# Fourteen pairs of k tiles as seven products instead of twelve, in the down projection of a hybrid decoder layer

## The chip, the cores and the metric

The kernel runs on one core of one Trainium2 chip. The metric is the device time of one execution in microseconds, as the median of several runs. The profile is one more execution, taken with the hardware profiler.

## The reference

One decoder layer on 256 tokens of width 2048, all in float32: a token mixer (mLSTM and RWKV-7 side by side), cross-attention into 256 memory tokens, and a convolutional GeGLU. Only the end of the layer bears on the change:

```python
def conv_glu_ffn(h, w_up, conv_w, conv_b, w_down):
    u = h @ w_up
    uc = conv_b + sum(conv_w[j] * shift_right(u, CONV_WIDTH - 1 - j) for j in range(CONV_WIDTH))
    gate, up = split_cols(uc, (D_FF, D_FF))
    return (jax.nn.gelu(gate, approximate=True) * up) @ w_down
...
x = x + rms_norm(conv_glu_ffn(h, ffn_w_up[l], ffn_conv_w[l], ffn_conv_b[l], ffn_w_down[l]), ffn_post_norm[l])
```

`w_down` is 8192 x 2048. The product with it, (256 x 8192) by (8192 x 2048), is the down projection.

## The kernel before, in words

**Matmuls in parts.** float32 operands are split into a high part and a low part of the type fp32r, and a product is made of three matmuls: high by high, low by high, high by low. A weight tile of 128 x 1024 (a chunk) comes by DMA into `raw`; ScalarE copies it to `wh` (L448), VectorE subtracts to get `wl = raw - wh` (L520). The activations of the down projection, two k tiles at a time, go the same way into `as` (`asplit`, L1911): ScalarE the high part, VectorE the low one.

**The down projection.** It is two blocks, 0 and 1, each of 1024 output columns and 64 chunks; a chunk is one k tile of 128 rows. Four PSUM banks hold the output: two tiles of 128 tokens by two halves of 512 columns. A chunk is 4 banks x 3 matmuls = 12 matmuls with 512 columns each.

**Pairs.** At the places listed in `SEVEN` (L1906) two chunks k and k+1 are taken together. Their work is a 2 x 2 by 2 x 2 product of blocks (two token tiles, two k tiles, two column halves), 8 block products or 24 matmuls when done plainly. `seven_products` (L532) does it with 7 products of sums and differences, 21 matmuls. Some of its products add into the block's own four banks (`tm` in the profile), others into four further ones (`more`), which `join_sums` adds up once per block, after the last pair. In this text a pair is named by its first chunk: pair 12 is chunks 12 and 13.

**The preparation of a pair.** `prepare` (L452) is a generator of six steps. Its weights b11, b12 (chunk k) and b21, b22 (chunk k+1) lie in `sraw`, one place for all pairs. What it makes, and what the profile calls it:

- step 1: `t` first half = b22 + b12, and a difference of activations (VectorE; both written to `end`, since `sraw`, the sums and other scratch share one piece of memory of that name)
- step 2: b12 = b12 - b11 in place, and two more differences of activations (VectorE, `end`)
- step 3: `t` second half = b22 + b12 (VectorE), high part of the activations `sa` (ScalarE)
- step 4: `t` third part = b21 - second half, low part of `sa` (VectorE), high part of `ts` (ScalarE, 1024 columns)
- step 5: low part of `ts` (VectorE), high part of `t4` (ScalarE, 512 columns)
- step 6: low part of `t4` (VectorE); the profile prints `t4` as `t`

The seven products read, in order: `as` by the first chunk, `as` by the second, `sa` by the first, `sa` by the second, `sa` by `ts` twice, `as` by `t4`. Since b12 is changed in place, the split of the pair's first chunk into `wh` and `wl` comes after step 2.

**What sets the order.** All instructions are written out in program order, and each engine works through its own in that order. In `work` (L577), for every chunk i: `feed.lo` sees to it that `wh` and `wl` exist up to chunk i+3 (L607 and L613; for a pair up to i+4), `ax` splits the activations of the next two chunks, `pair_loads` (L481) starts the loads of the next pair's weights, two chunks before the pair in front of it, `ahead_of_pairs` (L492) runs one step of `prepare` per chunk (more if it is behind), and only then come the chunk's matmuls. A preparation is due to start at chunk k - 6 (L401). `wh` and `wl` have five buffers each, `as` two, `raw` four. The gain of the last norm is loaded at chunk 24 of block 0 (`load_gain`, L1966).

Of the kernel before, what the change touches and what calls it, by code (L numbers as in the profile page):

```python
# [148 lines left out]
def layer(tc, d, dbg=None):  # L149
    with ExitStack() as ctx:  # L150
        ctx.enter_context(tc.manual_schedule())
        _layer(ctx, tc, tc.nc, d, dbg or (lambda n, t: None))


def _layer(ctx, tc, nc, d, dbg):
# [127 lines left out]
    class Stat:  # L283


        def __init__(self, name, tag="ysb1", sq="au", home=None):
            self.name, self.tag, self.sq, self.home = name, tag, sq, home
            self.rc = cp.tile([P, 2], F32, name=name + "_c")
            self.n = 0
            self.done = False  # L290
# [91 lines left out]
    def block(kind, srcs, xs, evac, before=None, cols=512, pool_=None, pre=None, bankwise=False, tail=0,  # L382
              two=False, wide=None, seven=None):


        blocks.append(dict(kind=kind, srcs=srcs, xs=xs, evac=evac, before=before, cols=cols,
                           pool=pool_ or acc, pre=pre, task=None, bankwise=bankwise, tail=tail, two=two, wide=wide is not None, xw=wide,
                           seven=seven))
        return blocks[-1]

    class Feed:
        def __init__(self):
            a, g = blocks[0]["srcs"], blocks[1]["srcs"]
            self.src = a[:LEAD] + [c for p in zip(a[LEAD:], g) for c in p] + g[len(a) - LEAD:]
            self.src += [s for b in blocks[2:] for s in b["srcs"]]
            n, self.pairs, self.preps = sum(len(b["srcs"]) for b in blocks[:2]), {}, []
            for b in blocks[2:]:
                if b["seven"]:
                    for k in b["seven"]["at"]:
                        self.pairs[n + k], self.pairs[n + k + 1] = 0, 1  # L400
                        self.preps.append([n + k - 6, self.prepare(n + k, k), n + k, []])  # L401
                n += len(b["srcs"])
            self.raw, self.st, self.nd, self.ns, self.nl, self.nop = {}, {}, 0, 0, 0, 0

# [321 lines left out]
    def W(name, blk):  # L726
        return [d[name][blk, c] for c in range(d[name].shape[1])]
# [1175 lines left out]
        fu = block("fm", W("w_fw", f - 6), fu_xs(f), fw_evac(f), cols=256, wide=lambda k: M["fx"][:, :, k])  # L1903

    M["as"], M["a4"], M["sa"], M["ts"] = {}, [], [], []
    SEVEN = [12, 20, 30, 38, 48, 56], [10, 18, 28, 36, 46, 54]  # L1906

    def acpair(e):
        return M["ac"][e // 16][:, e % 16:e % 16 + 2] if e < 32 else M["ac"][2 + (e - 32) // 8][:, e % 8:e % 8 + 2]
# [1 line left out]
    def asplit(k):  # L1911

        if k not in M["as"]:
# [5 lines left out]
            for j in range(2):  # L1919
                M["as"][k + j] = (a[:, 0, j], a[:, 1, j])  # L1920
            if e in SEVEN[k // 64]:
                M["a4"].append([a[:, i].rearrange("p k (t s) -> p (k t) s", t=2) for i in range(2)])
        return M["as"][k]

    def ax(n):
        def xs(k):
            kk = n * 64 + k
            if kk == 58:
                side.need(fu["task"])
            if kk == 2:  # L1930
                room()
            if kk == 24:
                load_gain()
            if k % 2 == 0:
                asplit(kk)
                if kk + 2 < 128 and (k < 62 or n == 0):
                    asplit(kk + 2)
            return M["as"].pop(kk)
        return xs
# [117 lines left out]
    def fd_ready(n):  # L2057
        return lambda: side.need(fd[0]["task"] if n else fu["task"])

    fd = []  # L2060
    for n in range(2):
        fd.append(block("tm", W("w_fd", n), ax(n), fd_evac(n), cols=1024, pool_=acc if n else aux,
                        tail=4 if n else 0, seven=dict(at=SEVEN[n], pool=aux if n else acc, ready=fd_ready(n))))
    run()
# [102 lines left out]
```

## Time and profile before

| what | value |
|---|---|
| median of 3 runs | 1797.09 us (1797.02 to 1797.45) |
| the profiled execution | 1796.52 us |
| its span, first to last instruction | 1794.7 us |
| granted TensorE clock, mean | 0.999 |
| TensorE busy | 1785.2 us, 99% of the span |
| VectorE busy | 1395.6 us, 78% |
| ScalarE busy | 1076.7 us, 60% |
| DMA read from HBM | 347.01 MB, 195 GB/s over the span |

A row of a timeline reads: start in us from the span's start, length in us, engine, line of the kernel, operation, output<-input, shapes, count, and in brackets how long the engine stood idle before it and who ended that. PE is TensorE (PEld its weight loads), DVE VectorE, ACT ScalarE, SP the engine that issues DMAs. L191 is the helper through which every matmul goes and L68 the one through which most of the work of DVE and ACT goes, so those instructions are told apart by their tiles.

### The profile page before, as it was taken

Reading aid. Unit: us, or ns where it says so; the run is one execution under the profiler, and the core shown is the slowest. Engines: PE = TensorE matmul, PEld = TensorE weight load, DVE = VectorE, ACT = ScalarE, POOL = GpSimd, SP = SyncE. Lnnn points to the kernel's source line nnn. Section 1 sums busy time; section 2 is a strip of 40 time slices with the busy share of each in tenths; the row PEclk is TensorE's granted clock in tenths of the full one; section 3 lists DMA queues with packets and bytes.
Section 4 is the critical chain, followed back from the end, with each engine's and each line's share of the span. In section 5 each row is a group of like instructions: output and inputs, shape, how many; then the busy total and the mean of one; then the engine's idle time right before and its main releaser. Section 6 shows DMA issues by size and latency. Waiting matters only on the chain.

```text
span 1794.7 us, 30098 instructions
## 1 busy us (share of the span) xinstructions
PE 1785.2 (99%) x11778; PEld 1629.7 (91%) x11778; DVE 1395.6 (78%) x2020; ACT 1076.7 (60%) x1616; POOL 28.9 (2%) x51
## 2 busy tenths in 40 slices
PE   9999999999999999999999999999999999999998
PEld 9999988888888999999999999999999998888887
DVE  7869995766665767778878777877777778888887
ACT  7576454654554666677566667666655655556554
POOL 0100000000100000000000000000000000000000
PEclk9999999999999999999999999999999999999999
DMA  8755564454556676656666666666666676767664
GB/s 283 206 170 186 164 190 146 125 180 144 200 188 211 227 243 186 190 150 197 208 203 198 203 209 192 199 206 204 199 200 209 192 229 213 227 186 227 209 209 129
DMA packets 99134, 351.59 MB, mean 196 GB/s; under 512 B 10896, under 2 KB 13968, under 8 KB 98864
## 3 DMA queue, kind: packets, MB, share of 16 engines
q1 hardware_dynamic: 97888, 347.38, 61.3%
q8 instruction: 92, 1.51, 0.3%
q0 software_dynamic: 384, 1.18, 0.2%
q10 hardware_dynamic: 720, 1.12, 0.2%
q14 instruction: 50, 0.41, 0.1%
HBM read 347.01 MB, written 2.10 MB: 195 GB/s over the span
## 4 chain that ended last, share of the span: by engine, by line
PE 99%; DVE 0%; DMA 0%; ACT 0%; issue 0%; SPq 0%; DVEq 0%; ACTq 0%
PE fm L191 55%; PE tm L191 37%; PE more L191 2%; PE gram L191 0%; PE Y L191 0%; PE lv L191 0%; DMA op<-in_op_dram 0%; PE X L191 0%; PE num L191 0%; PE zwa L191 0%; PE U L191 0%; PE gramA L191 0%; PE xo L191 0%; PE zg L191 0%; PE Tn L191 0%; PE mT L1472 0%
## 5 line engine op out<-in xcount | busy, mean ns | idle before, releaser
L520 DVE TENSOR_TENSOR wl<-raw,wh 128x1024 fp32r<-128x1024 f32 (+1 forms) x617 | 741.5, 1218 | 128.6 <-ACT wh L448 125.9
L448 ACT CAST wh<-raw 128x1024 fp32r<-128x1024 f32 (+1 forms) x617 | 633.6, 1044 | 112.7 <-PE tm L191 61.7
L191 PE MATMUL fm<-fx,wh 128*128 128x512 f32 (+1 forms) x2240 | 672.8, 364 | 0.6 <-DVE fx L68 0.4
L191 PE MATMUL fm<-fx,wl 128*128 128x256 f32 x2048 | 558.3, 273 | 0.0
L191 PEld LDWEIGHTS fm<-fx,wh 128*128 128x128 f32 x2240 | 409.3, 190 | 49.9 <-DVE fx L68 1.0
L191 PEld LDWEIGHTS fm<-fx,wl 128*128 128x128 f32 x2048 | 393.3, 192 | 0.0
L191 PE MATMUL tm<-wh,as 128*128 128x512 f32 x856 | 254.8, 379 | 0.0
L191 PE MATMUL tm<-wh,hx 128*128 128x512 f32 (+1 forms) x832 | 243.9, 378 | 1.4 <-ACT hx L68 1.4
L191 PEld LDWEIGHTS tm<-wh,as 128*128 128x128 f32 x856 | 161.7, 189 | 23.2 <-DVE as L68 0.3
L68 ACT COPY ul<-fm 128x256 f32<-128x256 f32 x128 | 44.9, 373 | 225.5 <-PE fm L191 225.5
L191 PE MATMUL fm<-hx,wh 128*128 128x256 f32 x1024 | 174.5, 277 | 0.0
L191 PEld LDWEIGHTS tm<-wh,hx 128*128 128x128 f32 x832 | 151.0, 189 | 21.8 <-POOL wh L507 1.6
L191 PE MATMUL tm<-wl,as 128*128 128x512 f32 x428 | 162.2, 379 | 0.0
L191 PEld LDWEIGHTS fm<-hx,wh 128*128 128x128 f32 x1024 | 155.6, 192 | 1.1
L191 PE MATMUL tm<-wl,hx 128*128 128x512 f32 (+1 forms) x416 | 152.5, 373 | 0.4 <-DVE wl L520 0.3
L68 DVE TENSOR_TENSOR us<-fm,ul 128x256 f32<-128x256 f32 x128 | 48.5, 420 | 131.2 <-ACT ul L68 131.2
L191 PE MATMUL fm<-hx,wl 128*128 128x256 f32 x512 | 140.8, 275 | 0.0
L68 ACT CAST as<-ac 128x512 fp32r<-128x512 f32 x64 | 39.4, 617 | 118.8 <-PE tm L191 118.8
L191 PEld LDWEIGHTS fm<-hx,wl 128*128 128x128 f32 x512 | 98.3, 192 | 0.0
L191 PEld LDWEIGHTS tm<-wl,as 128*128 128x128 f32 x428 | 80.9, 189 | 11.5
L191 PEld LDWEIGHTS tm<-wl,hx 128*128 128x128 f32 x416 | 77.5, 189 | 11.2 <-DVE wl L520 0.5
L191 PE MATMUL fm<-mg,wh 128*128 128x512 f32 (+1 forms) x320 | 84.9, 340 | 0.0
(406 smaller groups left out, 2114.8 us busy)
## 6 DMA issues: line engine op xcount, KB each, us to landing
raw<-in_w_fw_dram SPq DMA_DIRECT2D x232, 512.0 KB, 4.3
raw<-in_w_in_dram SPq DMA_DIRECT2D x160, 512.0 KB, 3.7
raw<-in_w_fd_dram SPq DMA_DIRECT2D x104, 512.0 KB, 4.1
raw<-in_w_br_dram SPq DMA_DIRECT2D x32, 512.0 KB, 4.2
raw<-in_w_mw_dram SPq DMA_DIRECT2D x24, 512.0 KB, 4.8
raw<-in_w_fu_dram SPq DMA_DIRECT2D x24, 512.0 KB, 4.0
end<-in_w_fd_dram SPq DMA_DIRECT2D x24, 512.0 KB, 3.6
raw<-in_w_mo_dram SPq DMA_DIRECT2D x8, 512.0 KB, 4.1
```

Of the source, the lines that this page charges most:

```text
L68: return f(out, *a, **k)
L191: pe.matmul(out, lhsT, rhs, start=start, stop=stop, skip_group_check=True)
L448: nc.scalar.copy(o, v)
L520: nc.vector.tensor_sub(o, v, h)
```

## The change

```diff
                     for k in b["seven"]["at"]:
                         self.pairs[n + k], self.pairs[n + k + 1] = 0, 1
-                        self.preps.append([n + k - 6, self.prepare(n + k, k), n + k, []])
+                        last = self.preps[-1][2] if self.preps else 0
+                        self.preps.append([max(n + k - 6, last + 1), self.prepare(n + k, k), n + k, []])
...
-    SEVEN = [12, 20, 30, 38, 48, 56], [10, 18, 28, 36, 46, 54]
+    SEVEN = [12, 18, 26, 34, 42, 48, 56], [10, 16, 24, 32, 40, 46, 54]
```

Each block has seven pairs instead of six. They lie 6 or 8 chunks apart instead of 8 or 10; 6 apart from the pair before are 18 and 48 in block 0, 16 and 46 in block 1. A preparation starts at chunk k - 6 as before, but not before the chunk behind the start of the pair in front. For a pair that is 6 apart that is k - 5; since k - 5 is the second chunk of the pair in front and has no turn of its own, the first two steps run together at k - 4, and the other four at k - 3, k - 2, k - 1 and k.

One line more stands in the file after it, so that from there on lines have a number higher by one (L520 becomes L521).

The order of the instructions shows what moves. First VectorE, in block 0, at the start of the preparation that follows pair 12. Before, from the `wl` of chunk 17 on (`end<-end` and `end<-ac` are steps 1 and 2, the `wl` between them is chunk 18's, the last one chunk 19's):

```order
L520 TENSOR_TENSOR wl_16088<-raw_16009,wh_16086 128x1024
L68 TENSOR_TENSOR end_15830<-end_15830 128x512
L68 TENSOR_TENSOR end_15830<-ac_10740 128x256
L520 TENSOR_TENSOR wl_16106<-raw_16030,wh_16104 128x1024
L68 TENSOR_TENSOR end_15830<-end_15830 128x512
L68 TENSOR_TENSOR end_15830<-ac_10740,end_15830 128x128 x2
L68 TENSOR_TENSOR as_16125<-ac_10740,as_16125 128x512
L520 TENSOR_TENSOR wl_16130<-raw_16056,wh_16128 128x1024
```

After, from the same place on (chunk 18 is now the first of the pair, so its `wl` reads `end`, where `sraw` lies):

```order
L521 TENSOR_TENSOR wl_16086<-raw_16009,wh_16084 128x1024
L68 TENSOR_TENSOR end_15830<-end_15830 128x512
L68 TENSOR_TENSOR end_15830<-ac_10740 128x256
L68 TENSOR_TENSOR end_15830<-end_15830 128x512
L68 TENSOR_TENSOR end_15830<-ac_10740,end_15830 128x128 x2
L521 TENSOR_TENSOR wl_16109<-end_15830,wh_16107 128x1024
L68 TENSOR_TENSOR end_15830<-end_15830 128x512
L68 TENSOR_TENSOR as_16129<-ac_10740,as_16129 128x512
L521 TENSOR_TENSOR wl_16135<-end_15830,wh_16133 128x1024
```

Steps 1 and 2 stand together, step 3 (the next `end<-end`) right behind the first `wl` of the pair.

Then VectorE at the end of the same preparation. Before, from the low part of `ts` for pair 20 on, to the two `wl` of chunks 23 and 24 (the pair's matmuls are issued behind `t4`):

```order
L68 TENSOR_TENSOR ts_16159<-end_15830,ts_16158 128x1024
L520 TENSOR_TENSOR wl_16202<-raw_16108,wh_16200 128x1024
L68 TENSOR_TENSOR t4_16161<-end_15830,t4_16160 128x512
L68 TENSOR_TENSOR as_16219<-ac_10740,as_16219 128x512
L520 TENSOR_TENSOR wl_16226<-raw_16132,wh_16222 128x1024
L520 TENSOR_TENSOR wl_16228<-raw_16154,wh_16224 128x1024
```

After, for pair 18, to the two `wl` of chunks 21 and 22:

```order
L521 TENSOR_TENSOR wl_16161<-raw_16054,wh_16159 128x1024
L68 TENSOR_TENSOR ts_16142<-end_15830,ts_16141 128x1024
L68 TENSOR_TENSOR as_16179<-ac_10740,as_16179 128x512
L521 TENSOR_TENSOR wl_16186<-raw_16088,wh_16182 128x1024
L521 TENSOR_TENSOR wl_16188<-raw_16111,wh_16184 128x1024
L68 TENSOR_TENSOR t4_16144<-end_15830,t4_16143 128x512
L68 TENSOR_TENSOR as_16214<-ac_10740,as_16214 128x512
```

The low part of `t4` stood ahead of the `as` and the two `wl`, and now stands behind them.

Last ScalarE, in the same stretch as the first place. Before, from the `wh` of chunk 17 on to the first `wh` of pair 20:

```order
L448 CAST wh_16086<-raw_16009 128x1024
L448 CAST wh_16104<-raw_16030 128x1024
L68 CAST as_16125<-ac_10740 128x512
L448 CAST wh_16128<-raw_16056 128x1024
L68 CAST sa_16135<-end_15830 128x512
L448 CAST wh_16150<-end_15830 128x1024
```

After, from the `wh` of chunk 17 on to the second `wh` of pair 18:

```order
L449 CAST wh_16084<-raw_16009 128x1024
L449 CAST wh_16107<-end_15830 128x1024
L68 CAST sa_16114<-end_15830 128x512
L68 CAST as_16129<-ac_10740 128x512
L449 CAST wh_16133<-end_15830 128x1024
```

The pair's first `wh`, which reads b12 after step 2, has come forward from behind `sa` to directly behind the `wh` of chunk 17.

## The prediction

> **What bounds the kernel now.** I read four views, in this order: the page of the profile, what TensorE (PE) waits for in the last 325 us (the down projection with its twelve pairs lies there), the timeline of PE around two pairs, and the timelines of VectorE (DVE) and ScalarE (ACT) over the same 20 us.
>
> ```profile
> span 1794.7 us, 30098 instructions
> ...
> PE 1785.2 (99%) x11778; PEld 1629.7 (91%) x11778; DVE 1395.6 (78%) x2020; ACT 1076.7 (60%) x1616; POOL 28.9 (2%) x51
> ```
>
> PE is busy for 99% of the span. In the window 1470 to 1794 us its whole list of waits is one row, and that one belongs to the very end, behind the last pair:
>
> ```profile
> PE sum L191 <- ACT turn L68: 0.9, 1, 0.9
> ```
>
> So in this stage PE never waits for a product's operands: every matmul taken away is worth its full spacing, and every new wait costs its full length. The spacing comes from the timeline of PE. Pair 12 of block 0 starts at 1494.00, pair 20 at 1514.08 (the third row is the seventh product of pair 20):
>
> ```profile
> 1494.00 0.59 PE L191 MATMUL more<-wh,as 128*128 128x512 f32 x2
> ...
> 1514.08 0.59 PE L191 MATMUL more<-wh,as 128*128 128x512 f32 x2
> ...
> 1517.96 0.81 PE L191 MATMUL tm<-t,as 128*128 128x512 f32 x3
> ```
>
> Between the two starts lie 21 matmuls of the pair and six chunks of 12, so 93 matmuls in 20.08 us: 0.216 us each, 2.59 us a chunk, 4.53 us a pair. Within a pair the seventh product starts 3.88 us after the start (1517.96 - 1514.08), and its third matmul, the only one that reads the low part of `t4`, two spacings later, at start + 4.31 us.
>
> DVE is the next busiest. Its timeline from pair 12 to pair 20, without the middle, shows what it does in a fixed order (start, length, output<-input, and in brackets its idle time and who ended it):
>
> ```profile
> 1499.39 0.69 DVE L68 TENSOR_TENSOR as<-ac,as 128x512 fp32r<-128x512 f32 x1 [1.17 <-ACT as L68]
> 1500.33 1.23 DVE L520 TENSOR_TENSOR wl<-raw,wh 128x1024 fp32r<-128x1024 f32 x1 [0.26 <-ACT wh L448]
> 1501.48 0.68 DVE L68 TENSOR_TENSOR end<-end 128x512 f32<-128x512 f32 x1
> 1502.08 0.42 DVE L68 TENSOR_TENSOR end<-ac 128x256 f32<-128x256 f32 x1
> 1502.41 1.22 DVE L520 TENSOR_TENSOR wl<-raw,wh 128x1024 fp32r<-128x1024 f32 x1
> 1503.55 0.69 DVE L68 TENSOR_TENSOR end<-end 128x512 f32<-128x512 f32 x1
> 1504.15 0.61 DVE L68 TENSOR_TENSOR end<-ac,end 128x128 f32<-128x128 f32 x2
> 1504.68 0.69 DVE L68 TENSOR_TENSOR as<-ac,as 128x512 fp32r<-128x512 f32 x1
> 1505.51 1.23 DVE L520 TENSOR_TENSOR wl<-raw,wh 128x1024 fp32r<-128x1024 f32 x1
> 1506.66 0.68 DVE L68 TENSOR_TENSOR end<-end 128x512 f32<-128x512 f32 x1
> ...
> 1510.75 1.22 DVE L520 TENSOR_TENSOR wl<-end,wh 128x1024 fp32r<-128x1024 f32 x1 [0.26 <-ACT wh L448]
> 1511.89 1.22 DVE L68 TENSOR_TENSOR ts<-end,ts 128x1024 fp32r<-128x1024 f32 x1
> 1513.03 1.22 DVE L520 TENSOR_TENSOR wl<-raw,wh 128x1024 fp32r<-128x1024 f32 x1
> 1514.16 0.68 DVE L68 TENSOR_TENSOR t<-end,t 128x512 fp32r<-128x512 f32 x1
> 1514.98 0.69 DVE L68 TENSOR_TENSOR as<-ac,as 128x512 fp32r<-128x512 f32 x1
> ```
>
> Three things are to be seen. Where nothing is waited for, the next instruction starts 1.14 us after one of 1024 columns (1511.89 to 1513.03) and 0.60 us after one of 512 (1501.48 to 1502.08). The last step of the preparation, the low part of `t4` (the row `t<-end,t`), ends at 1514.84, only 0.76 us after its pair started, and is read at 1518.39: a cover of 3.5 us. And DVE idles little: the bracketed rows shown add up to 1.69 us of slack in this 8-apart period.
>
> **What the change saves.** Each of the two added pairs takes 21 matmuls instead of 24: 3 x 0.216 = 0.65 us, for both 1.30 us. By the waits above nothing else hides in it, so the gross gain is 1.30 us.
>
> **What it adds by load.** Each added pair brings a preparation to DVE and ACT. On DVE, by the spacings: six instructions of 512 columns (3.60), one of 1024 (1.14), the 256 one (0.33, 1502.08 to 1502.41) and the pair of 128 ones (0.53, 1504.15 to 1504.68), 5.60 us. With six `wl` (6.84) and three `as` (1.80) a 6-apart period asks 14.24 us of DVE; PE takes 21 + 4 x 12 = 69 matmuls, 14.90 us. By load alone it fits, at 96%. ACT has less (in the page 60% against DVE's 78%).
>
> **What it moves.** In the four 6-apart pairs (18 and 48 in block 0, 16 and 46 in block 1) the preparation can begin only after the pair before, so it starts one DVE step denser and ends one chunk later: behind the two `wl` of the second and third chunk after the pair, and behind one more `as`. I follow DVE through it from pair 12 to pair 18. Up to the `wl` at 1500.33 nothing differs from the rows above.
>
> First step, at 1501.48: 512 columns (0.60), 256 columns (0.33), then at once `b12 - b11`, from 1502.41 to 1502.41 + 0.68 = 1503.09; the two small ones occupy DVE until 1502.41 + 0.60 + 0.53 = 1503.54. Here the change adds a wait. The next DVE instruction is now the `wl` of the pair's own first chunk. Its `wh` on ACT reads the `b12` just subtracted; in the order before, a `wl` stood between, and ACT came to that `wh` later anyway. ACT's rows give the hand-overs:
>
> ```profile
> 1504.44 1.04 ACT L448 CAST wh<-raw 128x1024 fp32r<-128x1024 f32 x1
> 1505.39 0.61 ACT L68 CAST sa<-end 128x512 fp32r<-128x512 f32 x1
> ...
> 1507.37 1.05 ACT L68 CAST ts<-end 128x1024 fp32r<-128x1024 f32 x1 [0.41 <-DVE end L68]
> ...
> 1514.33 0.62 ACT L68 CAST as<-ac 128x512 fp32r<-128x512 f32 x1 [2.14 <-PE tm L191]
> 1514.86 1.99 ACT L448 CAST wh<-raw 128x1024 fp32r<-128x1024 f32 x2
> ```
>
> From DVE's end to ACT's start: 1506.66 + 0.68 = 1507.34 to 1507.37, 0.03 us. From `wh`'s end to `wl`'s start: 1504.44 + 1.04 = 1505.48 to 1505.51, 0.03 us. So `wh` runs from 1503.12 to 1504.17 and `wl` starts at 1504.20; DVE has stood still for 0.66 us. On ACT `sa`, `as` and the second `wh` queue behind that wait; the first two end at the latest by 1504.17 + 0.61 + 0.62 = 1505.40, before DVE asks for them.
>
> Then come, ahead of the low part of `t4`: six of 1024 columns (three `wl` of the pair and the chunk behind it, `ts`, and two `wl` more) and five of 512 (three steps of the preparation counting `sa`, and two `as`): 6 x 1.14 + 5 x 0.60 = 9.84 us. It starts at 1514.04 and ends at 1514.72. Is DVE held up on that way by others? The second `as` needs ACT's, which PE releases at pair start + 0.25 (1514.33 - 1514.08) and which ends 0.62 later; the two `wh` behind it end at start + 2.77 (1514.86 + 1.99 - 1514.08). The pair now starts two chunks sooner, at 1514.08 - 5.18 = 1508.90, so these are ready at 1509.77 and 1511.67; DVE reaches them at 1511.16 and 1511.76 or later. DVE itself is the bound.
>
> PE wants that operand at 1508.90 + 4.31 = 1513.21. The hand-over from DVE to PE is seen at the start of the kernel:
>
> ```profile
> 10.23 0.76 DVE L520 TENSOR_TENSOR wl<-op,wh 128x592 fp32r<-128x592 f32 x1
> ...
> 11.05 0.52 PE L191 MATMUL tm<-wl,hx 128*128 128x296 f32 x2 [0.29 <-DVE wl L520]
> ```
>
> 10.99 to 11.05 is 0.06 us. So the 21st matmul starts at 1514.78, 1.57 us late. Behind it wait all matmuls of the next chunk, and ACT's next `as`, whose buffer the pair frees. The other operands are in time: `ts` low stands ahead of `t4` by itself, one `as` and two `wl`, so it starts at 1514.04 - 0.60 - 3 x 1.14 = 1510.02, ends at 1511.24 and is read by the 15th matmul at 1508.90 + 14 x 0.216 = 1511.92. After the pair DVE again waits for PE's release as at 1499.39, so no debt passes to the next pair, which is 8 apart and in the old order. The other three cases start alike; in block 1 the first step comes 7.47 us after pair 10's start, in block 0 7.48 after pair 12's:
>
> ```profile
> 1650.70 0.59 PE L191 MATMUL more<-wh,as 128*128 128x512 f32 x2
> ```
>
> ```profile
> 1658.17 0.68 DVE L68 TENSOR_TENSOR end<-end 128x512 f32<-128x512 f32 x1
> ```
>
> Four waits of 1.57 us are 6.28 us. Bounds for one of them: below, DVE has made up all its debt when the pair starts. Then `as` starts at start + 0.90 (1514.98), the first `wl` 0.94 later (1499.39 to 1500.33), `t4` two `wl` on, at 0.90 + 0.94 + 2.28 = 4.12; it ends at 4.80, PE goes on at 4.86, 0.55 us late. Above, no instruction overlaps the one before: with lengths instead of spacings the 11 instructions take 6 x 1.22 + 5 x 0.69 = 10.77 instead of 9.84, and a wait is 2.50 us. I take 1.57, since the rows show the overlap wherever nothing is waited for. [...]
>
> **What costs nothing.** The loads of the pair's weights keep their place against the pair before, and the later of the two goes out at 1491.93 for pair 20, and now for pair 18:
>
> ```profile
> 1491.93 0.33 SPq L487 DMA_DIRECT2D end<-in_w_fd_dram  x1
> ```
>
> ```profile
> end<-in_w_fd_dram SPq DMA_DIRECT2D x24, 512.0 KB, 3.6
> ...
> end<-in_fpg_dram SPq DMA_DIRECT2D x1, 1024.0 KB, 6.7
> ```
>
> It lands 3.6 us later, at 1495.5, and is first read at 1501.48: 6 us of cover. The load of the final gain (6.7 us) now stands directly ahead of the load for pair 34 on the SP queue; from there to pair 34's first step are four chunks, over 10 us, that hide it. Uncovered it could cost up to 6.7 us once.
>
> **The sum.** 6.28 - 1.30 = +4.98 us. On the profiled execution's own 1796.52 us (span 1794.7 and 1.8 around it) that is 1801.5; the median of the runs lies 0.57 above that execution, so 1797.09 + 4.98 = 1802.1 us, 0.28% more.
>
> **The rivals.** All are on the median. First, no wait at all: 1797.09 - 1.30 = 1795.8. For it speaks the load (14.24 of 14.90 us); against it the order, since `t4` is last in a queue that is released by the pair itself. It needs DVE 1.57 us sooner at the 21st matmul. This is the other side: not slower. Second, a short wait: DVE's debt is gone when the pair starts, 4 x 0.55 - 1.30 = +0.90, 1798.0. Against it: DVE has 0.66 us of slack in the period by load and loses as much at the `wh` that waits for `b12`. Third, the long wait: 4 x 2.50 - 1.30 = +8.70, 1805.8, if the denser order loses the overlap. Fourth, a load comes late behind the gain, up to 6.7 us more, 1808.8. That the change does not do what it says is no rival: the order of the instructions shows seven preparations in each block.
>
> **How the numbers follow.** Forecast 0.72, no wait 0.07, short wait 0.12, long wait 0.06, late load 0.03. The forecast's own range is 1.2 to 1.9 us a wait (a third of a microsecond for spacings read off rows), so 1800.6 to 1803.4. To leave out no more than 2 in 10 the range takes in the short wait: 1797.8 to 1803.8. 0.2% of the time, about what a measurement of this kernel can tell from no change, is 3.6 us. The forecast lies beyond it but for its lowest end (0.06 of the 0.72), so slower gets 0.66 + 0.06 + 0.03 = 0.75, within 0.2% 0.06 + 0.12 + 0.07 = 0.25, of which I leave 0.01 to a gain that I do not see: faster 0.01, same 0.24.
>
> **What would show it.** Right: in the profile after, PE's list of waits in this stage has a new row, PE `tm` waiting for DVE `t`, four times, 1.2 to 1.9 us each, at the 21st matmul of pairs 18, 48, 16 and 46 and nowhere else; ACT's `wh<-end` of these pairs waits for DVE `end`; `more<-ts` has 84 matmuls instead of 72, and the kernel six fewer in all. Wrong: no such row (then the first rival), waits under 0.8 us (the second), or a row with DMA or with `wl` as what PE waits for.

## The result, and the profile after

| | before | after |
|---|---|---|
| median | 1796.89 us (8 runs, 1796.51 to 1797.45) | 1802.41 us (8 runs, 1801.44 to 1802.60) |
| span of the profiled execution | 1794.7 us | 1800.8 us |
| TensorE matmuls | 11778 | 11772 |
| VectorE busy | 1395.6 us | 1405.9 us |

The ratio is 1.003, with a 95% interval of 1.0019 to 1.0041: slower by 5.52 us, where 4.98 was forecast. (The median of before is 0.2 us lower here than the one that the forecast was added to, because five more runs are in it.)

The list of what PE waits for from 1460 us on has one new row, its columns being who waited for whom, us in total, times, and the longest:

```profile
PE tm L191 <- DVE t L68: 5.8, 4, 1.4
PE sum L191 <- ACT turn L68: 0.9, 1, 0.9
```

Four waits for the low part of `t4`, and nothing else that is new. The timeline of PE in pair 18 of block 0 (its first product, the first two matmuls of the seventh, the third one, and the next chunk) shows what one of them costs:

```profile
1509.39 0.59 PE L191 MATMUL more<-wh,as 128*128 128x512 f32 x2
...
1513.28 0.59 PE L191 MATMUL tm<-t,as 128*128 128x512 f32 x2
1515.32 0.48 PE L191 MATMUL tm<-t,as 128*128 128x512 f32 x1 [1.45 <-DVE t L68]
1515.64 0.59 PE L191 MATMUL tm<-wh,as 128*128 128x512 f32 x2
```

Without a wait the third matmul would start at 1509.39 + 4.31 = 1513.70. It starts at 1515.32, 1.62 us late (the bracket says 1.45 because in the rows the two matmuls before it end at 1513.28 + 0.59 = 1513.87, later than 1513.70). The matmul after it comes 0.32 us on (1515.32 to 1515.64) instead of 0.216, so another 0.10 us go in starting again. The three other waits are the same row at other times, 1592.15, 1674.80 and 1751.62: pair 48, and pairs 16 and 46 of block 1.

The timeline of DVE through the same preparation, whole from its first step to `t4`:

```profile
1501.97 0.68 DVE L68 TENSOR_TENSOR end<-end 128x512 f32<-128x512 f32 x1
1502.57 0.42 DVE L68 TENSOR_TENSOR end<-ac 128x256 f32<-128x256 f32 x1
1502.91 0.69 DVE L68 TENSOR_TENSOR end<-end 128x512 f32<-128x512 f32 x1
1503.51 0.61 DVE L68 TENSOR_TENSOR end<-ac,end 128x128 f32<-128x128 f32 x2
1504.75 1.23 DVE L521 TENSOR_TENSOR wl<-end,wh 128x1024 fp32r<-128x1024 f32 x1 [0.63 <-ACT wh L449]
1505.89 0.69 DVE L68 TENSOR_TENSOR end<-end 128x512 f32<-128x512 f32 x1
1506.49 0.68 DVE L68 TENSOR_TENSOR as<-ac,as 128x512 fp32r<-128x512 f32 x1
1507.10 1.22 DVE L521 TENSOR_TENSOR wl<-end,wh 128x1024 fp32r<-128x1024 f32 x1
1508.23 0.68 DVE L68 TENSOR_TENSOR end<-end 128x512 f32<-128x512 f32 x1
1508.84 0.69 DVE L68 TENSOR_TENSOR sa<-end,sa 128x512 fp32r<-128x512 f32 x1
1509.44 1.22 DVE L521 TENSOR_TENSOR wl<-raw,wh 128x1024 fp32r<-128x1024 f32 x1
1510.57 1.22 DVE L68 TENSOR_TENSOR ts<-end,ts 128x1024 fp32r<-128x1024 f32 x1
1511.71 0.69 DVE L68 TENSOR_TENSOR as<-ac,as 128x512 fp32r<-128x512 f32 x1
1512.31 2.35 DVE L521 TENSOR_TENSOR wl<-raw,wh 128x1024 fp32r<-128x1024 f32 x2
1514.58 0.69 DVE L68 TENSOR_TENSOR t<-end,t 128x512 fp32r<-128x512 f32 x1
```

One bracket stands in it: DVE idles 0.63 us for the `wh` that reads `b12`. From there to `t4` no idle time is shown at all, 9.83 us of one instruction after the other. ACT's row for that `wh` is this:

```profile
1503.67 1.04 ACT L449 CAST wh<-end 128x1024 fp32r<-128x1024 f32 x1 [2.88 <-issue]
```

It starts 0.07 us after `b12 - b11` has ended (1502.91 + 0.69 = 1503.60). The profile names "issue" and not DVE here, so by this row alone the wait for `b12` is read off the times and not shown; the experiment "b12 first" tests it.

### The profile page after: what moved, and what is told of

It is laid out like the page before. It is cut to its first block, busy times and chain, and to the rows that moved or that the text cites. A ratio compares the mean times of both kernels' runs of the same rounds, so it can differ in the third digit from the quotient of the medians.

```text
span 1800.8 us, 30114 instructions
## 1 busy us (share of the span) xinstructions
PE 1786.3 (99%) x11772; PEld 1629.4 (90%) x11772; DVE 1405.9 (78%) x2040; ACT 1080.3 (60%) x1622; POOL 28.6 (2%) x51
## 5 line engine op out<-in xcount | busy, mean ns | idle before, releaser
L521 DVE TENSOR_TENSOR wl<-raw,wh 128x1024 fp32r<-128x1024 f32 (+1 forms) x613 | 737.1, 1218 | 126.5 <-ACT wh L449 123.5
L191 PE MATMUL tm<-wh,as 128*128 128x512 f32 x828 | 246.4, 379 | 0.0
L191 PEld LDWEIGHTS tm<-wh,as 128*128 128x128 f32 x828 | 156.4, 189 | 22.4 <-DVE as L68 0.3
L191 PE MATMUL tm<-wl,as 128*128 128x512 f32 x414 | 156.9, 379 | 0.0
```

Source lines behind the costliest of these rows:

```text
L191: pe.matmul(out, lhsT, rhs, start=start, stop=stop, skip_group_check=True)
L521: nc.vector.tensor_sub(o, v, h)
```

## The experiments

The theory, "order": the low part of `t4` comes late because of its place in DVE's queue, behind an `as` and two `wl` that the pair itself has set going, and each such pair costs some 1.72 us (1.62 and 0.10). The main rival, "load": seven preparations in a block are too much work for DVE, in whatever order. Each time below is the median of its runs, beside the kernel before on the same chip. The kernel before has a median of 1796.89, 1796.63 or 1796.79 us in the three series, so a time "against the changed kernel" is the difference of two differences, each from the kernel before in the same series; the changed kernel's own is 5.52 us.

**The last step moved ahead.** In `work`, for a pair's own chunk:

```diff
                 side.more = lambda: feed.hi(i + 2)
+                if pair:
+                    feed.ahead_of_pairs(i)
                 ahead = b["xs"](k)
```

> The changed kernel with one thing moved: at a pair's own chunk the last step of its preparation (low part of t4, one VectorE instruction of 512 columns) stands ahead of the as and the two wl instead of behind them. Theory 'order' (the wait comes because t4 stands last in VectorE's queue): t4 ends some 2.9 us sooner, PE's four waits for t are gone, and only the saving of two pairs is left: 1796.9 - 1.3 = 1795.6 us. Rival 'load' (seven preparations are too much work for VectorE, whatever the order): the work is the same, so the lateness moves to the as or wl behind, and the time stays near 1802.4 us.

Measured: 1795.35 us against 1796.63 (ratio 0.9993, 0.9984 to 1.0002). PE's waits in the stage are gone but for the one at the very end:

```profile
PE sum L191 <- ACT turn L68: 0.9, 1, 0.9
```

and DVE's timeline shows `t4` ahead of the `as`, ending at 1512.27, where in the changed kernel it ended at 1515.27:

```profile
1510.45 1.22 DVE L68 TENSOR_TENSOR ts<-end,ts 128x1024 fp32r<-128x1024 f32 x1
1511.58 0.69 DVE L68 TENSOR_TENSOR t<-end,t 128x512 fp32r<-128x512 f32 x1
1512.18 0.69 DVE L68 TENSOR_TENSOR as<-ac,as 128x512 fp32r<-128x512 f32 x1
1512.78 2.36 DVE L521 TENSOR_TENSOR wl<-raw,wh 128x1024 fp32r<-128x1024 f32 x2
```

DVE does the same work, with the same 0.62 us of idle time at the `wh`, and the `as` and `wl` that are now later are not missed by anyone. One instruction moved over three takes away the whole loss: 6.80 us against the changed kernel (5.52 + 1.28), where four waits of 1.72 are 6.88. "Load" falls.

**Twelve pairs, four of them close.**

```diff
-    SEVEN = [12, 18, 26, 34, 42, 48, 56], [10, 16, 24, 32, 40, 46, 54]
+    SEVEN = [12, 18, 30, 36, 48, 56], [10, 16, 28, 34, 46, 54]
```

> The changed kernel with twelve pairs as before, but four of them 6 apart (18 and 36 in block 0, 16 and 34 in block 1), the others 10 or 12 apart. Theory 'order': four waits as in the changed kernel and no saving, 1796.9 + 4 x 1.72 = 1803.8 us, PE waiting for t four times 1.45 us. Rival 'load': twelve preparations as before, so 1796.9 us and no wait, or at the most a part of it.

Measured: 1803.46 us against 1796.63 (ratio 1.0038, 1.0026 to 1.0051), 6.83 us more for four waits, 1.71 each. The list of waits is that of the changed kernel:

```profile
PE tm L191 <- DVE t L68: 5.8, 4, 1.4
PE sum L191 <- ACT turn L68: 0.9, 1, 0.9
```

With as many preparations as before and no saving, the whole loss is there. It hangs on the pairs that are 6 apart, not on how many pairs there are.

**The table alone.** The first half of the change is undone; the table stays.

```diff
-                        last = self.preps[-1][2] if self.preps else 0
-                        self.preps.append([max(n + k - 6, last + 1), self.prepare(n + k, k), n + k, []])
+                        self.preps.append([n + k - 6, self.prepare(n + k, k), n + k, []])
```

> Only the second half of the change: the table with fourteen pairs, while a preparation starts at chunk k - 6 as before, so for a pair that is 6 apart at the chunk of the pair in front. Its steps then end at chunk k - 1. Theory 'order': no wait for t at any pair, 1795.6 us, and the wh that waited for b12 - b11 waits less or not. Rival 'load': as much work in the same time, so PE waits for something of VectorE as before, near 1802.4 us.

Measured: 1795.50 us against 1796.63 (0.9993, 0.9984 to 1.0002), and no wait for `t`: PE's list in the stage is again the single row for `sum`. So the lower bound on the start is the half of the change that costs. The part of the expectation that speaks of `wh` was wrong. On ACT `sa` now stands ahead of that `wh`, and waits for DVE first:

```profile
1503.12 0.62 ACT L68 CAST sa<-end 128x512 fp32r<-128x512 f32 x1 [2.42 <-DVE end L68]
1503.64 1.04 ACT L449 CAST wh<-end 128x1024 fp32r<-128x1024 f32 x1
```

so DVE stands still longer than in the changed kernel:

```profile
1504.71 1.22 DVE L521 TENSOR_TENSOR wl<-end,wh 128x1024 fp32r<-128x1024 f32 x1 [1.03 <-ACT wh L449]
...
1511.06 0.69 DVE L68 TENSOR_TENSOR t<-end,t 128x512 fp32r<-128x512 f32 x1
1511.66 0.69 DVE L68 TENSOR_TENSOR as<-ac,as 128x512 fp32r<-128x512 f32 x1
```

1.03 us instead of 0.63. It costs nothing, because `t4` is again ahead of the `as`: it ends at 1511.75, and the pair, which starts at 1509.29, reads it at 1509.29 + 4.31 = 1513.60, so 1.85 us are to spare. The stand-still matters only where it is handed on to something that PE waits for.

**The last step done twice.**

```diff
             dve.tensor_sub(t4[1], t[:, 1024:], t4[0])
+            dve.tensor_sub(t4[1], t[:, 1024:], t4[0])
```

> The changed kernel with the last step of every preparation done twice (the same subtraction into the same place). Theory 'order': in the four pairs that are 6 apart the wait grows by the spacing of one 512-column instruction, 4 x 0.60 = 2.4 us, to 1804.8 us, PE waiting four times about 2.05 us; in the ten others it is covered. Rival 'load': all fourteen are felt, 14 x 0.60 = 8.4 us, to 1810.8 us.

Measured: 1811.48 us against 1796.63 (1.0081, 1.0067 to 1.0095). "Order" had expected 1804.8 and missed by 6.7 us. The time looks like that of "load", but the profile says otherwise. There are four waits and not fourteen:

```profile
PE tm L191 <- DVE t L68: 8.7, 4, 2.2
PE sum L191 <- ACT turn L68: 0.9, 1, 0.9
```

Each grew by 0.72 us (1.45 to 2.17) and not by 0.60: in DVE's timeline the two subtractions into the same place take 1.41 us together, so the second starts 0.73 us after the first (1.41 - 0.68), about when the first ends. That is 2.9 us of 9.33 against the changed kernel (14.85 - 5.52). The rest is in the granted clock, the share of its full speed at which TensorE ran. The busy time by stages of 2 us behind the first wait (PE, PEld, DVE, ACT and POOL busy with their counts, then the granted clock, DMA share, GB/s):

```profile
1515.00:1517.00 2.00, 1.86 (x7) 1.59 (x8) 0.72 (x2) 1.29 (x2) 0.00 (x0) 0.81 0.94 344
1517.00:1519.00 2.00, 2.00 (x7) 1.55 (x6) 1.75 (x3) 1.23 (x2) 0.00 (x0) 0.50 0.15 61
1519.00:1521.00 2.00, 2.00 (x9) 1.74 (x8) 2.00 (x4) 0.00 (x0) 0.00 (x0) 0.83 0.74 199
1521.00:1523.00 2.00, 2.00 (x11) 1.74 (x11) 0.70 (x3) 0.48 (x1) 0.00 (x0) 1.00 0.75 190
```

and the same stages in the changed kernel:

```profile
1515.00:1517.00 2.00, 1.68 (x8) 1.49 (x9) 0.72 (x2) 1.10 (x2) 0.00 (x0) 1.00 0.77 244
1517.00:1519.00 2.00, 2.00 (x11) 1.76 (x10) 1.75 (x3) 1.41 (x2) 0.00 (x0) 1.00 0.69 268
```

At half the clock the rows hold 0.76, 2.00 and 0.68 us (0.19, 0.50 and 0.17 missing out of 0.50, times 2 us), 3.4 us in all; in the middle one 7 matmuls run where the changed kernel has 11. The second wait follows the first by 1594.38 - 1515.13 = 79.25 us, in the changed kernel by 1592.15 - 1515.32 = 76.83: 2.42 us more, 0.72 from the wait and 1.70 from the clock. Four times that is 9.7 us; by the medians it is 9.33.

**b12 first.** In `prepare`, the first activation difference goes behind `b12 - b11`:

```diff
-            dve.tensor_sub(f[:, 0:2], x[:, 1:2].broadcast_to((P, 2, P)), x[:, 0:4:3])
             yield
             dve.tensor_sub(b12, b12, b11)
+            dve.tensor_sub(f[:, 0:2], x[:, 1:2].broadcast_to((P, 2, P)), x[:, 0:4:3])
```

> The changed kernel with b12 - b11 ahead of the first activation difference in the preparation (the two swap places across the border of steps 1 and 2; the same instructions in all). ScalarE's wh of the pair's first chunk then gets b12 0.33 us sooner (the 256-column instruction no longer stands ahead). Theory 'chain' (VectorE's stand-still at that wh is handed on to t4, instruction by instruction): the four waits shrink by 0.33 us each, from 1.45 to 1.12, and the time by 1.3 us to 1801.1. Rival 'covered' (VectorE would wait for ScalarE or PE further on anyway): waits stay 1.45 and the time 1802.4 us.

Measured: 1801.46 us against 1796.79 (1.0026, 1.0016 to 1.0036), 4.67 us slower instead of 5.52, so 0.85 less than the changed kernel, and each wait 1.23 us:

```profile
PE tm L191 <- DVE t L68: 4.9, 4, 1.2
```

DVE's timeline shows why it is 0.22 and not 0.33 us:

```profile
1501.48 1.41 DVE L68 TENSOR_TENSOR end<-end 128x512 f32<-128x512 f32 x2
1502.81 0.42 DVE L68 TENSOR_TENSOR end<-ac 128x256 f32<-128x256 f32 x1
...
1504.05 1.22 DVE L521 TENSOR_TENSOR wl<-end,wh 128x1024 fp32r<-128x1024 f32 x1 [0.16 <-ACT wh L449]
```

The two subtractions, now side by side, take 1.33 us to the next start instead of 1.20. The second overwrites what the first reads, and starts 0.73 us after it (1.41 - 0.68) instead of 0.60. The `wl` starts 2.57 us after the first step instead of 2.78 (1504.75 - 1501.97), and those 0.21 us come out at PE: four times that is 0.84. So the first link of the chain, from `b12` over ACT to `wl`, does reach PE.

**Sixteen pairs.** The table alone, with eight pairs in each block:

```diff
-    SEVEN = [12, 18, 26, 34, 42, 48, 56], [10, 16, 24, 32, 40, 46, 54]
+    SEVEN = [12, 18, 24, 30, 36, 44, 50, 56], [10, 16, 22, 28, 34, 42, 48, 54]
```

and the preparation at k - 6 as in "the table alone".

> Eight pairs a block, 6 or 8 apart, each preparation started at chunk k - 6 as in the kernel before (no lower bound). Theory 'order': with t4's low part ahead of as and wl no pair waits, even where five 6-apart pairs follow each other, and four pairs more than before save 4 x 3 x 0.216 = 2.6 us: 1794.0 us. Rival 'load': a 6-apart period asks VectorE for 14.24 of 14.90 us besides its waits for ScalarE, so a debt grows from pair to pair and PE waits at the later ones: 1797 us or more.

Measured: 1794.14 us against 1796.79 (0.9985, 0.9976 to 0.9994), so faster than both kernels, by 2.65 us against before, where 2.6 was expected. PE waits for nothing in the stage but at its end:

```profile
PE sum L191 <- ACT turn L68: 0.9, 1, 0.9
```

There is no growing debt even with four 6-apart periods in a row.

**Waits between 1.45 and 2.17 us.** In two kernels, each run twice, the first 256 or the first 384 columns of `t4`'s low part are written again (`w` is that number):

```diff
             dve.tensor_sub(t4[1], t[:, 1024:], t4[0])
+            dve.tensor_sub(t4[1][:, 0:w], t[:, 1024:1024 + w], t4[0][:, 0:w])
```

> The changed kernel with the first 256 of the 512 columns of t4's low part written a second time, so that each of the four waits grows from 1.45 to about 1.90 us. Doubling the whole step gave waits of 2.17 us, and behind each of them a granted clock of 0.50 for some 3.4 us, which the changed kernel with 1.45 us does not show. If the clock falls only from 2 us on, this one keeps 1.00 and takes 1802.4 + 4 x 0.45 = 1804.2 us; if it falls already at 1.9 us, 4 x 1.6 more, 1810.6 us.

> As the run with 256 columns, but with the first 384 written a second time: waits of about 2.03 us. With the clock kept, 1802.4 + 4 x 0.58 = 1804.7 us; with the clock at 0.50 behind each wait, 1811.1 us.

Measured: with 256 columns 1810.35 us in one run and 1804.29 in the other; with 384 columns 1810.01 and 1806.47. Both answers of the expectation occur. In the profiled executions (the 1810.35 and the 1810.01) the waits are 1.90 and 2.04 us:

```profile
PE tm L191 <- DVE t L68: 7.6, 4, 1.9
```

```profile
PE tm L191 <- DVE t L68: 8.1, 4, 2.0
```

With 256 columns all four are followed by a clock near 0.5. With 384 columns the first is not, and the second is, though they are equally long; the first 2 us behind each:

```profile
1516.00:1518.00 2.00, 2.00 (x10) 1.76 (x11) 0.69 (x1) 1.50 (x3) 0.00 (x0) 1.00 0.73 291
1593.50:1595.50 2.00, 2.00 (x6) 1.60 (x7) 0.69 (x1) 1.58 (x3) 0.00 (x0) 0.55 0.87 285
```

So the length alone does not decide. The times agree: 1804.29 is the sum without any fall of the clock (1804.2 expected), 1806.47 lies about one such fall above that with 384 columns (1804.7 expected).

The falls themselves are alike. With 256 columns the rows of 2 us behind the first wait have a clock of 0.74, 0.50, 0.91 and then 1.00; as above, with 0.26, 0.50 and 0.09 missing out of 0.50, that is 3.40 us at half the clock. Done in the same way for all eleven falls of the three executions, it is 3.40 to 3.44 us each time. The 24 waits for `t` of the six profiles that have any, by length:

| waits | clock behind |
|---|---|
| four of 1.23 us (b12 first) | no fall by its time: 4.67 us slower than before, the changed kernel's 5.52 less four times 0.21 |
| eight of 1.45 us (changed kernel; twelve pairs, four of them close) | 1.00 in the changed kernel; no fall by its time in the other (1.71 us a wait) |
| four of 1.90 us (256 columns) | 0.50 (mean clock of the execution 0.996) |
| the first with 384 columns, 2.04 us | 1.00 |
| the three others with 384 columns, 2.03 and 2.04 us | 0.50 (mean 0.996) |
| four of 2.17 us (last step twice) | 0.50 (mean 0.995) |

In these executions no wait of up to 1.45 us was followed by a fall, and eleven of the twelve of 1.90 us or more were; no wait lies in between. Why one wait of 2.04 us had no fall is not shown. Nor is it shown why the second execution with 256 columns had none: it has no profile, only its time and a mean clock of 1.0.

## Why the prediction was right

- **The saving**, 1.30 us for two pairs. Supported, not measured by itself: the two kernels with fourteen pairs and no wait are 1.28 and 1.13 us faster than before, but their intervals include no change. Sixteen pairs save 2.65 us by an interval that does not, for four pairs, and the forecast's working gives 2.59.
- **Load**, 96% of a 6-apart period. It fits, as forecast; sixteen pairs show it.
- **The hand-over at b12.** Forecast 0.66 us of standing still, measured 0.63. The forecast wanted ACT's row to name DVE there, and it names no engine; the times fit, and "b12 first" shows the link.
- **DVE's chain** from the first `wl` of the pair to `t4`. Forecast 9.84 us, measured 9.83. The spacings of before hold, and lengths (10.77 us, the upper bound) would have been wrong. In the timeline after, the `as` behind the low part of `ts` starts 1.14 us after it (1510.57 to 1511.71), at a length of 1.22.
- **The wait.** Forecast 1.57 us, measured 1.62. Where the four are, and that there are no others, was as forecast. So was the count of `more<-ts`, 84 matmuls instead of 72.
- **What was missing**: the 0.10 us that PE loses at the restart. 4 x (1.62 + 0.10) - 1.30 = 5.58 us against 5.52 measured; the forecast's 4.98 is short by those four restarts and four times 0.05.
- **The clock** was not in the forecast, and no reason was given for leaving it out. It stayed at 1.00 behind waits of 1.45 us in the profile after, and no run of the changed kernel lies above 1802.60. With half a microsecond more in each wait it could have added some 6 us, as the runs with 256 columns show. That it added nothing here is luck as far as the forecast goes.
- **The load of the gain** ahead of pair 34's weights cost nothing: PE has no wait there.

## What to carry to other kernels

Where an engine works through a queue written in program order, ask of each late operand what stands ahead of it and what released that; here being busy for 96% of a period was harmless, and standing behind three instructions that the consumer itself releases was not. Where a new step seems to need a later start, check whether it does: here the preparation could start at the old place, and the pair's last operand would not have moved. A short wait on TensorE costs its length only as long as the clock holds: here eleven of twelve profiled waits of 1.90 to 2.17 us were followed by some 3.4 us at a clock of 0.50, which cost 1.5 to 1.8 us on top, and none of the twelve of 1.23 or 1.45 us was.

## What the runs showed of the hardware

A wait of TensorE of 1.45 us left the granted clock at full speed eight times of eight, in two executions (1.00 in the rows behind it in the changed kernel; by its time, 1.71 us a wait, in the one with twelve pairs). At 1.90 us it fell to 0.50 four times of four in one execution and, by its time (1804.29 us) and its mean clock (1.0), never in another; at 2.03 to 2.04 us three times of four; at 2.17 us four times of four. Each fall lasted 3.40 to 3.44 us by the rows of 2 us and cost 1.5 to 1.8 us: 1.52 with 256 columns ((1810.35 - 1804.29) / 4), 1.70 with the last step twice (from the distance of two waits), 1.77 with 384 ((1810.01 - 1804.7) / 3, from the expected sum). Waits of the same length went both ways; what decides between them was not shown.

Behind a wait of 1.45 us the matmul after the delayed one started 0.32 us after it instead of 0.216. On DVE, independent instructions of 512 columns started 0.60 us apart at a length of 0.68 (1501.97 to 1502.57 in the changed kernel); two of which the second overwrote what the first read or wrote started 0.73 us apart ("b12 first", "the last step done twice").
